# The memory's keys and values of a decoder layer: sums of squares as a row per head, roots spread by four row products, a written-out order

## The chip, the cores and the metric

The kernel runs on one core of a Trainium2 chip, in one launch. The metric is the device time of that launch in microseconds (us). A core has TensorE (PE, matrix products into PSUM banks), VectorE (DVE), ScalarE (ACT) and GpSimd (POOL) for elementwise work, and SyncE (SP), which issues most of the DMA transfers; some are issued by ACT. Each engine works through its own list of instructions in order, and semaphores tie the lists together.

## The reference, cut to what matters

One step of a decoder layer for a prompt of 1024 tokens and eight sample sequences of 4 tokens. The layer has a mixer (gated MLP beside latent attention), a cross-attention into 256 memory tokens with 4 heads of 128, and a gated convolutional FFN. The change lies where the memory's keys and values are made, between the sample's latent attention and the mixer's output projection:

```python
def mem_kv(mem, g_mem_in, w_mk, w_mv, g_mk):
    hm = rms_norm(mem, g_mem_in)                        # over 1024 features
    k = rms_norm((hm @ w_mk).reshape(n, m, 4, 128), g_mk)   # over 128, per head
    v = (hm @ w_mv).reshape(n, m, 4, 128)
# both are outputs, too; around it stand
s = masked scores of the sample's queries over 4096 cached latents, softmax, o = p @ latents
out = concat(rms_norm(a_out), rms_norm(b_out)) @ w_o
```

All is float32. A product that must keep float32's accuracy is made of three: each operand is split into a high part (a cast by ACT) and a low part (the difference, by DVE), and PE adds high*high, low*high and high*low.

## The kernel before

`phase2b` does the sample's attention over 8 batches of 16 pairs of cache pages (128 pairs, numbered by `n`). For a pair PE makes scores, ACT squares them, DVE and POOL form norms. A batch's softmax runs in 14 steps (`batch_softmax`, `r` = 0 to 13) behind its scores, then comes its product with the latents ("PV", `quad_pv`, 67 records of 257 columns) and its sums over pairs (`fold`, `oo`, `batch_out`, `batch_close`), which leave the attention's output as `olT`. `steps(n0, n1)` issues what is due in steps `n0` to `n1 - 1`, `at(n, pos, f)` adds to it; `late` holds those softmax steps of the last batch that are due behind the last score (`last` = 128).

Up to the last score the order on PE, ACT, DVE and POOL is written out by hand. Behind it only SP's is (`manual_schedule(engines={E.SP})`); a list scheduler that works with estimated costs orders the other four engines. `mem_kv` is a generator that the stage advances between pieces of the last batch's softmax. Its work, in this order:
- four heads of keys: `b` (PSUM) gets 24 records of 256 columns for a head, from 8 slices of the head's weights (`wk0`, then `stream`ed tiles `hi`, `lo`) and 8 slices of the memory tokens (`mh`, `ml`). The memory's raw tokens lie in two `ck` tiles. Head 0's loop splits them, ACT the high parts and DVE the low ones, 128x256 at a time. ACT copies each head to `kr` and its squares to `sq`;
- the memory's own sums of squares: ACT squares the raw tokens, DVE reduces 128x1024 to 128x256 twice (`acc`);
- the values `v0`, `v1` (PSUM), each 4 x 6 records of 512 columns;
- one-column products of `sq` and `acc` with a column of ones into `st`: a token is a partition there, and a head a column. DVE makes the tokens' root `rt` (128x2) and the heads' factors `r` (128x8);
- for each head two diagonal 128x128 tiles (`diag` = `ident` times a column of `r`) and their products with ones (L1658), which spread the factors along a row over all partitions; DVE multiplies `kr` with that (L1659), and ACT issues the writes of `o_mk`. ACT scales the values to `vf` by `rt` and issues `o_mv`; `vf` is one buffer.

Then `mixed` loads the rest of the mixer's output `mix` from memory and splits it into `mx1h`/`mx1l` and `mx2h`/`mx2l` (columns 384 to 767 and the rest), and `out_proj` makes the products with `w_o` in chunks `chunk(m, c)`: `m` is one of 8 slices of output features, `c` one of three ranges of tokens (384, 384, 288 columns), 24 records each. `end` makes 32 small products of `olT` with `wuv`, whose normalised result `n` is transposed by PE (`o<-ident,n`, in `mixed_sample`) and needed for `c` = 2. The ring `raw` of three 512 KB buffers takes the raw weights and the raw mixes, each one's load waiting until the splits of the one three places before are done.

Of the kernel before, what the change touches and what calls it, by code (L numbers as in the profile page):

```python
# [13 lines left out]
P = 128  # L14
# [139 lines left out]
class Net:  # L154
# [83 lines left out]
    def rsqrt_steps(self, p, out, ss, scale, e=None, eps=EPS):  # L238
# [5 lines left out]
        x, q, y, a = (self.t(p, [P, n], d, f"rq{k}{n}", 2 if n < 100 else 1)[:w] for k, d in (("x", F32), ("h", F32), ("y", I32), ("a", F32)))  # L244
# [5 lines left out]
        for k in range(2):  # L250
            yield
            o = out if k else y
            if e is nc.vector:
# [6 lines left out]
                e.scalar_tensor_tensor(o, q, 5.0, y, ALU.add, ALU.mult)  # L260
# [918 lines left out]
    def phase2b(self):  # L1179
# [50 lines left out]
        at(last - 4, 3, lambda: self.split(*wk0, raws[0].rearrange("p (k n) -> p k n", k=8)))  # L1230
        for b in range(NB):
# [3 lines left out]
            for r, (k, pos) in enumerate(((12, 0), (13, 0), (14, 0), (14, 3) if b == NB - 1 else (15, 0), (15, 0) if b == NB - 1 else (15, 3), (16, 0), (17, 0), (17, 3), (18, 2), (19, 2), (20, 0), (21, 2), (22, 3))):  # L1235
                f = lambda b=b, r=r: self.batch_softmax(p, ppt, st[b], r, b == NB - 1)
                if n + k <= last:
                    at(n + k, pos, f)
                else:
                    late.append(f)  # L1240
# [15 lines left out]
        def steps(n0, n1):  # L1256
            for n in range(n0, n1):
# [27 lines left out]
                if 0 <= n < last:  # L1285
                    rope = (Q + 1, quads[Q + 1], st[(Q + 1) // 8]) if n % 2 and Q + 1 < NB * 8 else None
                    for f in self.pair_score(p, pp, n, quads[n // 2], st[n // 16], rope):
                        at(n + 1, -1, f)
# [12 lines left out]
        with tc.manual_schedule(engines={E.SP}):  # L1301
# [5 lines left out]
            mem = self.mem_kv(raws, wk0)  # L1307
            for f in late[:3]:
                f()
            next(mem)  # L1310
            steps(last + 1, last + 4)
            for _ in range(5):
                next(mem)
            steps(last + 4, last + 7)
            for f in late[3:]:
                f()
            for _ in range(6):
                next(mem)
            steps(last + 7, last + 16 + LAG)
            for _ in mem:  # L1320
                pass
# [140 lines left out]
    def batch_softmax(self, p, pp, s, r, final):  # L1462
# [28 lines left out]
        elif r == 4:  # L1491
            s["m"] = self.t(p, [P, 2, 32], F32, "mx", 2)
            peak(0, 0, 24)
        elif r == 5:
            s["it"] = norms(24, 32, nc.gpsimd if final else nc.vector)
# [6 lines left out]
        elif r == 8:  # L1502
            scale(nc.vector, 24, 32)
# [10 lines left out]
        elif r == 11:  # L1514
# [4 lines left out]
            if final:  # L1519
                self.less(nc.vector, s)  # L1520
# [20 lines left out]
    def batch_out(self, p, s, part, pp=None, final=False):  # L1541
        nc = self.nc
        if part == 0:
            s["oo"] = self.t(p, [P, 257], F32, "oo", 2)
            nc.scalar.copy(s["oo"], s["o"])
# [33 lines left out]
    def mem_kv(self, raws, wk0):  # L1579
# [7 lines left out]
        mh, ml = (self.t(p, [P, 8, 256], FR, x) for x in ("mh", "ml"))  # L1587
        acc = [self.t(p, [P, 256], F32, f"acc{z}") for z in range(2)]
        mr = [r.rearrange("p (k n) -> p k n", k=4) for r in raws[1:3]]
        xs = [(mh[:, k], ml[:, k]) for k in range(8)]  # L1590
        kr, sq = [], []

        for h in range(4):
            w = wk0 if h == 0 else self.stream(I["w_mk"][h], 8, raw=raws[3].rearrange("p (k n) -> p k n", k=8) if h == 1 else None)
            if h == 1:
                self.behind(self.cast, cast)
            yield
            ps = self.t(pp, [P, 512], F32, "b", 2)[:, :256]
            pairs = ((0, 0), (1, 0)), ((0, 1),)
            for z in pairs if h == 0 else (((0, 0), (0, 1)), ((1, 0),)):  # L1600
                for k in range(8):
                    if h == 0 and z is pairs[0]:
                        cast = self.split(*xs[k], mr[k // 4][:, k % 4], self.col("g_mem_in", k))
                    for a, e in z:
                        nc.tensor.matmul(
                            ps, w[a][:, k], xs[k][e], start=z[0] == (0, 0) and a + e + k == 0, stop=len(z) == 1 and k == 7
                        )
                    if h == 0 and z is pairs[0] and k % 2:
                        yield
            kr.append(self.t(p, [P, 256], F32, "kr", 4))  # L1610
            nc.scalar.copy(kr[h], ps)
            sq.append(self.t(p, [P, 256], F32, "sq", 4))
            nc.scalar.activation(sq[h], ps, AF.Square)
            yield
        for x, s2 in zip(mr, acc):
            nc.scalar.activation(x, x, AF.Square)
            nc.vector.tensor_reduce(s2, x.rearrange("p k n -> p n k"), AX.X, ALU.add)
        yield
        av = [self.t(pp, [P, 512], F32, f"v{i}") for i in range(2)]

        def values(k):
            wh, wl = (x.rearrange("p k n -> p (k n)").rearrange("p (k n) -> p k n", k=2) for x in self.stream(I["w_mv"][k // 2], 8))
            for i in range(2):
                t = slice(i * P, i * P + P)
                x = self.mm3(av[i], [tuple(x[:, t] for x in xs[k + e]) for e in range(2)],
                             [(wh[:, e], wl[:, e]) for e in range(2)], first=k == 0, last=k == 6)
                if k == 4 and i == 0:
                    self.behind(x, self.spread)

        values(0)  # L1630
        yield
        values(2)
        yield
        for h in range(4):
            for i in range(2):
                nc.tensor.matmul(st[:, 2 * h + i : 2 * h + i + 1], sq[h][:, i * P : i * P + P], self.ones[:, :1], start=True, stop=True)
# [4 lines left out]
        r2 = self.t(p, [P, 2], F32, "r2")  # L1641
        r = self.t(p, [P, 4, 2], F32, "r")
        four = lambda x: x.unsqueeze(1).broadcast_to([P, 4, 2])
        self.rsqrt(p, rt, st[:, 8:10], 1.0 / 1024)
        nc.vector.tensor_tensor(r2, rt, rt, ALU.mult)
        nc.vector.tensor_tensor(r, st[:, :8].rearrange("p (h i) -> p h i", h=4), four(r2), ALU.mult)
        rf = r.rearrange("p h i -> p (h i)")
        self.rsqrt(p, rf, rf, 1.0 / 128)
        nc.vector.tensor_tensor(r, r, four(rt), ALU.mult)
        yield  # L1650
        values(4)
        yield
        for h in range(4):
            bc = self.t(pp, [P, 512], F32, "b", 2)[:, :256]
            for i in range(2):
                dg = self.t(p, [P, P], F32, "diag", 3)
                nc.vector.tensor_scalar(dg, self.ident, r[:, h, i : i + 1], None, ALU.mult)
                nc.tensor.matmul(bc[:, i * P : i * P + P], self.ones, dg, start=True, stop=True)  # L1658
            nc.vector.scalar_tensor_tensor(kr[h], kr[h], self.col("g_mk"), bc, ALU.mult, ALU.mult)  # L1659
            nc.scalar.dma_start(O["o_mk"][h], kr[h])  # L1660
            if h == 1:
                yield
        yield
        values(6)
        for i in range(2):
            vf = self.t(p, [P, 512], F32, "vf")
            x = nc.scalar.activation(vf, av[i], AF.Copy, scale=rt[:, i : i + 1])
            if i:
                self.behind(x, self.exp)
            nc.scalar.dma_start(O["o_mv"][i * P : i * P + P], vf)  # L1670
        self.close("pskv")
# [926 lines left out]
```

## Time and profile before

| what | value |
|---|---|
| median of 3 runs | 1815.08 us (1813.99 to 1815.76) |
| the profiled execution | 1815.49 us, of which the profile's span is 1813.8 us |
| PE busy | 1791.1 us, 99% of the span |
| DVE, ACT, POOL busy | 74%, 51%, 39% |
| mean granted clock of TensorE | 0.997 |

The span runs from the first to the last instruction; 1.7 us of the execution's time lie outside. Positions below are us from the span's start. The stage of the change lies between 845.9 us (the last scores) and about 907 us (the first products of the projection's third range of tokens), and PE is the busiest engine there as everywhere. A record is one matrix instruction; it is shown with its full length, though the next starts before it ends, so the cost of a record in a row of them is the distance of two starts.

### The profile page before, as it was taken

Reading aid. Unit: us, or ns where it says so; the run is one execution under the profiler, and the core shown is the slowest. Engines: PE = TensorE matmul, PEld = TensorE weight load, DVE = VectorE, ACT = ScalarE, POOL = GpSimd, SP = SyncE. Lnnn points to the kernel's source line nnn. Section 1 sums busy time; section 2 is a strip of 40 time slices with the busy share of each in tenths; the row PEclk is TensorE's granted clock in tenths of the full one; section 3 lists DMA queues with packets and bytes.
Section 4 is the critical chain, followed back from the end, with each engine's and each line's share of the span. In section 5 each row is a group of like instructions: output and inputs, shape, how many; then the busy total and the mean of one; then the engine's idle time right before and its main releaser. Section 6 shows DMA issues by size and latency. Waiting matters only on the chain.

```text
span 1813.8 us, 39386 instructions
## 1 busy us (share of the span) xinstructions
PE 1791.1 (99%) x14259; PEld 1696.6 (94%) x14259; DVE 1347.4 (74%) x2778; ACT 921.0 (51%) x1931; POOL 705.9 (39%) x858
## 2 busy tenths in 40 slices
PE   9999999999999999999999999999999999999999
PEld 8999777769999999998899989999999999999999
DVE  7864777667678777787644678988888888878664
ACT  7335676766556555565434567433333333344442
POOL 1021656534455445453033001476677767400000
PEclk9999999999999999999999999999999999999999
DMA  8101354558876666663655255122222222584242
GB/s 324 48 18 62 118 184 129 164 164 229 226 206 191 190 186 194 178 190 125 188 157 195 97 169 181 58 95 83 72 71 83 72 83 83 163 319 150 88 147 78
DMA packets 153044, 261.06 MB, mean 144 GB/s; under 512 B 20881, under 2 KB 97394, under 8 KB 152850
## 3 DMA queue, kind: packets, MB, share of 16 engines
q1 hardware_dynamic: 151986, 257.50, 45.8%
q8 instruction: 113, 1.85, 0.5%
q10 hardware_dynamic: 864, 1.05, 0.2%
q14 instruction: 81, 0.66, 0.1%
HBM read 212.66 MB, written 45.82 MB: 143 GB/s over the span
## 4 chain that ended last, share of the span: by engine, by line
PE 77%; DVE 5%; ACT 2%; DMA 1%; issue 1%; POOL 1%; SPq 1%; DVEq 0%; ACTq 0%; POOLq 0%
PE s L185 22%; PE d L185 12%; PE b L185 8%; PE E L185 7%; PE F L185 7%; PE X L185 7%; PE A L185 3%; PE o L1046 2%; PE o L1537 2%; PE tp L1031 1%; PE tp L185 1%; PE s L1422 1%; PE tp L984 1%; PE v L185 1%; PE t L185 0%
## 5 line engine op out<-in xcount | busy, mean ns | idle before, releaser
L185 PE MATMUL s<-w2h,ch 128*128 128x256 f32 x1018 | 302.1, 297 | 0.0
L185 PE MATMUL s<-w2h,cl 128*128 128x256 f32 x1018 | 293.6, 288 | 0.0
L185 PE MATMUL s<-w2l,ch 128*128 128x256 f32 x1018 | 293.1, 288 | 0.0
L185 PEld LDWEIGHTS s<-w2h,ch 128*128 128x128 f32 x1018 | 191.6, 188 | 3.3 <-issue 2.9
L185 PEld LDWEIGHTS s<-w2h,cl 128*128 128x128 f32 x1018 | 191.4, 188 | 0.4 <-DVE rqa L257 0.4
L185 PEld LDWEIGHTS s<-w2l,ch 128*128 128x128 f32 x1018 | 191.8, 188 | 0.0
L1458 DVE TENSOR_REDUCE ss<-sq 128x16 f32<-128x1024 f32 x128 | 155.2, 1213 | 29.2 <-ACT sq L1455 29.1
L1407 POOL TENSOR_TENSOR cl<-cT,ch 128x512 fp32r<-128x512 f32 x64 | 86.2, 1346 | 197.8 <-ACT ch L1403 192.0
L1455 ACT ACTIVATE sq<-s 128x512 f32<-128x512 f32 x128 | 76.4, 597 | 72.3 <-PE s L185 72.2
L200 ACT CAST a<-brb 128x528 fp32r<-128x528 f32 x77 | 48.9, 634 | 114.7 <-PE d L185 111.2
L1452 ACT ACTIVATE sq<-s 128x512 f32<-128x512 f32 x128 | 76.6, 599 | 50.4 <-PE s L185 41.2
L201 DVE TENSOR_TENSOR a<-brb,a 128x528 fp32r<-128x528 f32 x77 | 54.3, 706 | 59.1 <-ACT a L200 58.8
L185 PE MATMUL d<-a,w 128*128 128x264 f32 x768 | 95.5, 285 | 1.2 <-DVE G L2366 1.2
L185 PEld LDWEIGHTS d<-a,w 128*128 128x128 f32 x768 | 94.3, 188 | 1.4 <-issue 1.4
L2233 POOL TENSOR_TENSOR lo<-s,hi 128x1024 fp32r<-128x1024 f32 x20 | 64.2, 3208 | 45.7 <-ACT hi L2232 45.7
L2289 ACT COPY a<-A 128x264 f32<-128x264 f32 x43 | 16.1, 375 | 120.6 <-PE A L185 114.3
L185 PE MATMUL mm<-wlo,xh 128*128 128x256 f32 (+3 forms) x272 | 77.1, 286 | 0.1
L185 PE MATMUL mm<-whi,xh 128*128 128x256 f32 (+3 forms) x272 | 77.1, 285 | 0.0
L185 PE MATMUL mm<-whi,xl 128*128 128x256 f32 (+3 forms) x272 | 76.9, 287 | 0.0
L1403 ACT CAST ch<-cT 128x512 fp32r<-128x512 f32 x128 | 73.6, 628 | 0.2 <-issue 0.2
L2355 POOL TENSOR_TENSOR cv<-cv,row 128x1056 f32<-128x1056 f32 x22 | 65.1, 2958 | 21.0 <-ACT cv L2354 21.0
L185 PE MATMUL d<-a,hi 128*128 128x264 f32 x552 | 72.0, 285 | 0.0
(802 smaller groups left out, 6371.3 us busy)
## 6 DMA issues: line engine op xcount, KB each, us to landing
cT<-cT SPq DMA_DIRECT2D x256, 160.0 KB, 2.7
ck<-ck SPq DMA_DIRECT2D x256, 144.0 KB, 3.5
raw<-w_up SPq DMA_DIRECT2D x44, 512.0 KB, 3.6
wsumd<-wsum SPq DMA_DIRECT2D x26, 512.0 KB, 3.5
actd<-cv SPq DMA_DIRECT2D x44, 264.0 KB, 2.4
brb<-actd SPq DMA_DIRECT2D x44, 264.0 KB, 5.6
wsum<-w_down SPq DMA_DIRECT2D x22, 512.0 KB, 3.7
raw<-wsumd SPq DMA_DIRECT2D x20, 512.0 KB, 3.7
```

The costliest lines, as they stand in the source:

```text
L185: x = self.nc.tensor.matmul(out, l, r, start=first and i == 0, stop=last and i == len(seq) - 1)
L200: first = {"act": nc.scalar.copy, "pool": nc.gpsimd.tensor_copy, "dve": nc.vector.tensor_copy}[eng](hi, src)
L201: low = lambda: nc.vector.tensor_tensor(lo, src, hi, ALU.subtract)
L1046: nc.tensor.matmul(u["o"][g : g + 64, o : o + m * P], s["v"][:, j, h % 4], th[:, z * P : (z + m) * P], start=j == 0, stop=b == len(banks) - 1,
L1403: nc.scalar.copy(d["h"][:, k], src[k])
L1407: (nc.vector if k else nc.gpsimd).tensor_tensor(d["l"][:, k], src[k], d["h"][:, k], ALU.subtract)
L1452: nc.scalar.activation(sq[:, 0], ps[:, :, n0 : n0 + 256], AF.Square)
L1455: nc.scalar.activation(sq[:, 1], pt.rearrange("p (e d) -> p e d", e=2), AF.Square)
L1458: yield lambda: nc.vector.tensor_reduce(s["ss"][:, g0 : g0 + 2].rearrange("p e (z h) -> p z e h", z=2), sq.rearrange("p z e (h d) -> p z e ...
L1537: nc.tensor.matmul(s["o"][j * 32 : j * 32 + 32], S[:, q * 4 + j], d["ck"][:, j, :257], start=q == 0 and j > 0, stop=q == 7)
L2233: eng.tensor_tensor(lo, src, hi, ALU.subtract)
L2355: nc.gpsimd.tensor_tensor(cv, cv, row, ALU.mult)
```

## The change

- **Order.** In `mem_kv` PE, ACT and DVE follow the order in which the code is written, as SP does; in `mixed` and the first chunks of `out_proj` PE does. `mem_kv` is no longer advanced from outside but calls the softmax steps itself (`late`, and `six`, `seven` for the steps behind the last score).
- **The memory's split.** The first four of the eight slices are split between the last scores (`mem_split`, at step `last - 1`), into a tile of the softmax (`S`) and one of the ring `ck`; the other four follow the last score. The value banks are allotted ahead of `b`, so that head 0's bank is one that pair 126 had used, not the last pair.
- **Sums.** Three DVE adds (1024, 512 and 256 wide) in place of the two reduces. The squares of a head are summed by a product with 32 columns of ones, so that a head is a group of 32 partitions of `st` and a token a column (eight products, the second four adding the memory's own sums, scaled by `unit`). Four one-column records stay for `rt`.
- **Roots and their spreading.** The reciprocal root, 11 DVE operations, is taken of 128x256 (in the four `sq` tiles) instead of 128x8. The row of a head is then spread over the partitions by one product with a column of `ident` repeated 128 times: four products in place of eight diagonals and eight products.
- **Around it.** The one-column sum of batch 6's output and its four fold records come behind head 0 and head 1. The last batch's norms go from POOL to DVE. The loads of the mixes go ahead of those of `xT`. The splits of the second weights of `w_o` are tied behind the exponential (high) and the roots (low). The `wuv` products come behind the whole `chunk(0, 1)`.

```diff
-    def mem_kv(self, raws, wk0):
+    def mem_kv(self, raws, wk0, m0, late, six, seven):
...
+        av = [self.t(pp, [P, 512], F32, f"v{i}") for i in range(2)]
+        ml, mh = (self.t(p, [P, 4, 256], FR, x) for x in ("ml", "mh"))
...
+        xs = m0 + [(mh[:, k], ml[:, k]) for k in range(4)]
...
+        def add():
+            q = [x.rearrange("p k n -> p (k n)") for x in mr]
+            for n in (1024, 512, 256):
+                x, y = q if n == 1024 else (q[0][:, :n], q[0][:, n : 2 * n])
+                nc.vector.tensor_tensor(q[0][:, :n], x, y, ALU.add)
+            return q[0][:, :256]
...
+        for f in six[:3]:
+            f()
+        for k in range(4, 8):
+            self.split(*xs[k], mr[1][:, k % 4], self.col("g_mem_in", k))
+        head(0)
+        late[0]()
+        load(1)
...
+        lows[6]()
+        acc = add()
+        load(7)
+        lows[7]()
+        self.less(nc.vector, self.final)
+        values(2, 0, 1)
+        for z in range(2):
+            for h in range(4):
+                nc.tensor.matmul(
+                    st[32 * h : 32 * h + 32, :256], self.ones[:, :32], acc if z else sq[h], start=z == 0, stop=z == 1
+                )
         for i in range(2):
-            for z in range(2):
-                nc.tensor.matmul(st[:, 8 + i : 9 + i], acc[z][:, i * P : i * P + P], self.ones[:, :1], start=z == 0, stop=z == 1)
+            nc.tensor.matmul(st[:, 256 + i : 257 + i], acc[:, i * P : i * P + P], self.ones[:, :1], start=True, stop=True)
+        late[8]()
+        values(3, 0, 1)
         rt = self.t(p, [P, 2], F32, "rt")
...
+        r = sq[3]
+        for _ in self.rsqrt_steps(p, r, st[:, :256], 1.0 / 128, eps=EPS * EPS, room=sq):
+            pass
+        self.rows = self.root
+        self.rsqrt(p, rt, st[:, 256:258], 1.0 / (1024 * unit * unit))
+        seven()
         for i in range(2):
             vf = self.t(p, [P, 512], F32, "vf")
...
+            nc.scalar.activation(vf, av[i], AF.Copy, scale=rt[:, i : i + 1])
             nc.scalar.dma_start(O["o_mv"][i * P : i * P + P], vf)
+        bc = [self.t(pp, [P, 512], F32, "b", 2) for _ in range(2)]
+        bc = [x[:, e * 256 : e * 256 + 256] for x in bc for e in range(2)]
+        for h in range(4):
+            nc.tensor.matmul(bc[h], self.ident[:, 32 * h : 32 * h + 1].broadcast_to([P, P]), r, start=True, stop=True)
+        for h in range(4):
+            nc.vector.scalar_tensor_tensor(kr[h], kr[h], self.col("g_mk"), bc[h], ALU.mult, ALU.mult)
+            nc.scalar.dma_start(O["o_mk"][h], kr[h])
...
+        def rest():
+            tail[2]()
+            load((2,))
...
-        end()
-        for m in range(10):
+        E = mybir.EngineType
+        with self.tc.manual_schedule(engines={E.SP, E.PE}):
+            chunk(0, 0)
+            rest()
+            chunk(0, 1)
+            end()
+        for m in range(1, 10):
```

On PE, where the scores end: the first piece is of before, the second of after. The `s` rows are the last pair's scores, `b<-mh,wk0` (after: `b<-S,wk0`) head 0's products.

```order
5482 L185 MATMUL s_2094_14316<-w2h_1705,cl_14192 128x256
5483 L1561 MATMUL m_14456<-fold_1084_5705,oo_14408 128x32 x2
5484 L1605 MATMUL b_14410<-mh_14394,wk0h_5692 128x256
5485 L1605 MATMUL b_14410<-mh_14394,wk0l_5693 128x256
5486 L1605 MATMUL b_14410<-mh_14394,wk0h_5692 128x256
```

```order
5481 L185 MATMUL s_2096_14325<-w2h_1705,cl_14192 128x256
5482 L1619 MATMUL b_14402<-S_14309,wk0h_5692 128x256
5483 L1619 MATMUL b_14402<-S_14309,wk0l_5693 128x256
5484 L1619 MATMUL b_14402<-S_14309,wk0h_5692 128x256
...
5499 L1619 MATMUL b_14402<-ml_14380,wk0h_5692 128x256 x4
5500 L1558 MATMUL m_14438<-oo_14392,fold_1084_5705 128x1
5501 L1619 MATMUL b_14447<-S_14309,hi_14428 128x256
```

Head 0 now follows the scores directly and begins with slices that were split before; the fold records have gone behind it.

On ACT, behind the values: before, then after. `vf` are the scaled values, `mx1h` the high parts of the mix, `oo` and `olT` the copies of the last batch's output.

```order
958 L1667 ACTIVATE vf_14775<-v_2136_14617,rt_14667 128x512
959 L1670 DMA o_mv<-vf_14775 128x512
960 L1667 ACTIVATE vf_14778<-v_2137_14618,rt_14667 128x512
961 L1670 DMA o_mv<-vf_14778 128x512
962 L204 ACTIVATE mx1h_14793<-raw_14809,cols_58 128x384 x2
...
970 L1660 DMA o_mk<-kr_14575 128x256
971 L1562 COPY olT_5703<-m_14835 128x16x4
```

```order
961 L204 ACTIVATE mx1h_14756<-raw_14791,cols_58 128x384 x2
962 L204 ACTIVATE mx1h_14756<-raw_14797,cols_58 128x384 x2
963 L1707 ACTIVATE vf_14724<-v_2101_14378,rt_14663 128x512
964 L1708 DMA o_mv<-vf_14724 128x512
965 L1707 ACTIVATE vf_14727<-v_2102_14379,rt_14663 128x512
966 L1708 DMA o_mv<-vf_14727 128x512
967 L1715 DMA o_mk<-kr_14443 128x256
968 L1715 DMA o_mk<-kr_14501 128x256
969 L1715 DMA o_mk<-kr_14537 128x256
970 L1715 DMA o_mk<-kr_14571 128x256
971 L1571 COPY olT_5703<-m_14768 128x16x4
```

The scaled values stood ahead of the mix's eight high parts and stand behind them now, so that both `vf`, both `o_mv` and all four `o_mk` lie directly ahead of `olT`.

On DVE, the same place in after; the 11 operations of the roots in the `sq` tiles (L250 to L264) end right ahead of this piece, which before held the `diag` tiles, one `kr` and the mix's low halves (`mx1l`) in turn.

```order
1549 L259 SCALAR_TENSOR_TENSOR rqa_2153_14678<-rqy_2152_14677 128x2
1550 L207 SCALAR_TENSOR_TENSOR mx1l_14757<-raw_14791,cols_58,mx1h_14756 128x384
1551 L262 TENSOR_TENSOR rqa_2153_14678<-rqa_2153_14678,rqx_2150_14675 128x2
1552 L207 SCALAR_TENSOR_TENSOR mx1l_14757<-raw_14791,cols_58,mx1h_14756 128x384
1553 L263 SCALAR_TENSOR_TENSOR rqh_2151_14676<-rqa_2153_14678 128x2
1554 L264 SCALAR_TENSOR_TENSOR rt_14663<-rqh_2151_14676,rqy_2152_14677 128x2
1555 L1714 SCALAR_TENSOR_TENSOR kr_14443<-kr_14443,cols_58,b_14730 128x256
1556 L1714 SCALAR_TENSOR_TENSOR kr_14501<-kr_14501,cols_58,b_14730 128x256
1557 L1714 SCALAR_TENSOR_TENSOR kr_14537<-kr_14537,cols_58,b_14731 128x256
1558 L1714 SCALAR_TENSOR_TENSOR kr_14571<-kr_14571,cols_58,b_14731 128x256
```

The tokens' root `rt` and, behind it, the four `kr` now follow the low halves of the third load of the mix (`raw_14791`).

## Rows read from the trace of the kernel before

**Rows 1.** The page's head and its first part: busy time and share.

```profile
span 1813.8 us, 39386 instructions
...
PE 1791.1 (99%) x14259; PEld 1696.6 (94%) x14259; DVE 1347.4 (74%) x2778; ACT 921.0 (51%) x1931; POOL 705.9 (39%) x858
```

**Rows 2.** Waits of PE, 843 to 908 us: engine, line, tile, releaser, total us.

```profile
PE b L1605 <- DVE S L1454: 1.5, 1, 1.5
PE b L1658 <- DVE diag L1657: 1.0, 3, 0.6
PE m L1508 <- DVE mx L1505: 0.4, 1, 0.4
```

**Rows 3.** Stretches: length, busy PE, PEld, DVE, ACT, POOL; then TensorE's granted clock.

```profile
867.90:870.50 2.60, 2.60 (x24) 2.52 (x22) 1.30 (x2) 1.23 (x2) 0.00 (x0) 1.00 0.83 251
871.00:874.40 3.40, 3.40 (x9) 2.65 (x9) 2.44 (x13) 1.08 (x1) 0.00 (x0) 0.50 0.44 118
```

**Rows 4.** Timeline of PE: start, length, instruction, [idle before].

```profile
845.89 0.28 PE L185 MATMUL s<-w2h,cl 128*128 128x256 f32 x1
846.01 0.53 PE L1561 MATMUL m<-fold,oo 128*128 128x32 f32 x4
848.06 0.36 PE L1605 MATMUL b<-mh,wk0h 128*128 128x256 f32 x1 [1.52 <-DVE S L1454]
...
852.34 0.28 PE L1605 MATMUL b<-mh,hi 128*128 128x256 f32 x1
```

**Rows 5.** Timeline of ACT: the memory's high parts in head 0.

```profile
846.79 3.31 ACT L204 ACTIVATE mh<-ck,cols 128x256 fp32r<-128x256 f32 x8
```

**Rows 6.** Timeline of PE: the diagonal products, and `out_proj` to `wuv`.

```profile
881.84 1.36 PE L1658 MATMUL b<-diag,ones 128*128 128x128 f32 x8
...
885.83 0.42 PE L185 MATMUL b<-mx0h,hi 128*128 128x384 f32 x1
...
890.60 0.34 PE L185 MATMUL b<-mx1h,hi 128*128 128x384 f32 x1
...
893.99 1.97 PE L1328 MATMUL m<-wuv,olT 128*32 128x64 f32 x32
...
906.61 0.43 PE L1751 MATMUL o<-ident,n 32*128 32x32 f32 x4
```

**Rows 7.** Timeline of PE: 256-column float32 products elsewhere in the kernel.

```profile
208.24 0.65 PE L1046 MATMUL o<-pth,v 128*64 128x256 f32 x4
...
1035.79 0.64 PE L1861 MATMUL st<-qsq,ones 128*32 128x256 f32 x8
```

**Rows 8.** Groups of DVE operations 256 wide: count, busy us, mean ns.

```profile
L1555 DVE TENSOR_SCALAR oo<-oo,rd 128x256 f32<-128x256 f32 x7 | 2.5, 352 | 0.2
...
L1476 DVE TENSOR_TENSOR S<-S,ss 128x256 f32<-128x256 f32 x7 | 2.9, 415 | 0.0
...
L207 DVE SCALAR_TENSOR_TENSOR ml<-ck,cols,mh 128x256 fp32r<-128x256 f32 x3 | 1.3, 487 | 0.0
```

**Rows 9.** Timeline of DVE: a weight's low half, a mix's low half.

```profile
876.25 1.23 DVE L201 TENSOR_TENSOR lo<-raw,hi 128x1024 fp32r<-128x1024 f32 x1 [2.42 <-ACT hi L200]
...
885.22 0.61 DVE L207 SCALAR_TENSOR_TENSOR mx1l<-raw,cols,mx1h 128x384 fp32r<-128x384 f32 x1
```

**Rows 10.** Timeline of ACT and its DMA issues (ACTq), 876 to 905 us.

```profile
876.53 0.69 ACT L1667 ACTIVATE vf<-v,rt 128x512 f32<-128x512 f32 x1 [0.32 <-PE v L185]
...
879.63 0.69 ACT L1667 ACTIVATE vf<-v,rt 128x512 f32<-128x512 f32 x1 [2.41 <-DMA o_mv<-vf]
...
883.11 0.34 ACTq L1660 DMA_DIRECT2D o_mk<-kr  x1
...
890.79 0.19 ACT L1562 COPY olT<-m 128x64 f32<-128x64 f32 x1
...
904.74 0.71 ACT L1748 ACTIVATE n<-raw,r 32x512 f32<-32x512 f32 x1
```

**Rows 11.** DMA issues, 860 to 900 us: size, median us to landing.

```profile
raw<-mix SPq DMA_DIRECT2D x4, 384.0 KB, 3.7
```

More of the change, by code (lines that the diff above doesn't have):

```diff
@@ L1299, in phase2b @@
             steps(-10, last + 1)
-        with tc.manual_schedule(engines={E.SP}):
+        with tc.manual_schedule(engines={E.SP, E.PE, E.Activation, E.DVE}):
             self.close("ps3")
@@ L1306, in phase2b @@
             self.wp = self.open("w", bufs=3, side="right")
[L1307 to L1321, printed above, removed]
+            six = [lambda n=n: steps(last + n, last + n + 1) for n in range(1, 7)]
+            self.mem_kv(raws, wk0, m0, late, six, lambda: steps(last + 7, last + 16 + LAG))
         self.close("p3")
@@ L1502, in batch_softmax @@
         elif r == 8:
-            scale(nc.vector, 24, 32)
+            if final:
+                if "part" not in s:
+                    s["part"] = scale(nc.vector, 24, 32)
+                    self.peak = lambda: peak(0, 0, 24)
+                    return
+            else:
+                scale(nc.vector, 24, 32)
             peak(1, 24, 33)
@@ new lines, in mem_kv, with load @@
+        kr, sq, w, lows, ps = [], [], {0: wk0}, {}, {}
+        unit = float(np.float32((EPS / 8) ** 0.5))
+        pair = lambda x: x.rearrange("p k n -> p (k n)").rearrange("p (k n) -> p k n", k=2)
+        def load(j):
+            self.lows = []
+            if j == 1:
+                w[j] = self.stream(None, 8, raw=raws[3].rearrange("p (k n) -> p k n", k=8))
+            else:
+                w[j] = self.stream(I["w_mk"][j] if j < 4 else I["w_mv"][j - 4], 8)
+            lows[j] = self.lows.pop()
+            self.lows = None
@@ L1614, in mem_kv @@
[L1614 to L1623, printed above, removed]
-                t = slice(i * P, i * P + P)
[L1625 to L1636, printed above, removed]
+            nc.scalar.activation(sq[h], ps[h], AF.Square)
+        def values(j, *ii):
+            wh, wl = (pair(x) for x in w[j + 4])
+            for i in ii:
+                t = slice(i * P, i * P + P)
+                self.mm3(av[i], [tuple(x[:, t] for x in xs[2 * j + e]) for e in range(2)],
+                         [(wh[:, e], wl[:, e]) for e in range(2)], first=j == 0, last=j == 3)
@@ new lines, in mem_kv @@
+        lows[1]()
+        load(2)
+        for f in six[3:5]:
+            f()
+        keep(0)
+        head(1)
+        late[1]()
+        lows[2]()
+        load(3)
+        for x in mr:
+            nc.scalar.activation(x, x, AF.Square, scale=unit)
+        late[2]()
+        late[3]()
+        late[4]()
+        lows[3]()
+        six[5]()
+        keep(1)
+        head(2)
+        load(4)
+        lows[4]()
+        self.peak()
+        keep(2)
+        head(3)
+        load(5)
+        keep(3)
@@ new lines, in mem_kv @@
+        values(0, 0, 1)
+        lows[5]()
+        late[4]()
+        load(6)
+        values(1, 0)
+        late[5]()
+        late[6]()
+        values(1, 1)
+        late[7]()
+        lows[6]()
[9 more added lines that the diff above has]
+                )
@@ L1644, in mem_kv @@
[L1644 to L1662, printed above, removed]
@@ L1722, in mixed, with load @@
         ws = {}
-        with self.tc.manual_schedule(engines={mybir.EngineType.SP}):
-            for c, (o, n) in enumerate(CH):
-                if c == 2:
-                    for f in tail:
-                        f()
+        def load(cs):
+            for c in cs:
+                o, n = CH[c]
                 if c < 2:
                     ws[c] = self.stream(I["w_o"][c], 8)
+                    if c:
+                        self.behind(self.cast, self.exp)
+                        self.behind(self.low, self.rows)
                 for k in range(0, 8 if c else 0, 2):
@@ L2554, in build @@
     pso = N.open("pso", space=PSUM)
-    N.out_proj(pso, po, mxs, ws, xh, xl, r3, end)
+    N.out_proj(pso, po, mxs, ws, xh, xl, r3, rest, end)
     N.x = xh, xl
```

82 lines of the change are left out of this document (41 added, 41 removed).

## The prediction

> **What bounds the kernel now.** I read the page's busy shares first: PE is busy for 1791.1 of 1813.8 us [rows 1], so a gain must shorten PE's own list or fill one of its idle stretches, and work taken from another engine counts only where PE waits for it. PE's waits come next: between 843 and 908 us it waits 1.5 us for DVE before head 0, 1.0 us for the diagonals and 0.4 us for the softmax's peak [rows 2]; a wait not listed there (for `olT`, `n`, any part of the mix) is none in the kernel before. Then the clock by stretches: at 867.9 to 870.5 PE does 24 one-column records in 2.60 us at full clock, and from 871.0 to 874.4 the granted clock is 0.50, that is 1.2 instead of 2.4 GHz, while PE is busy throughout [rows 3]. So the stage loses time in four places, all of which the change touches. The order of the changed kernel then says what the other engines put in their place.
>
> **PE's own path, in the time of the trace before.**
> - *To head 2.* The last score starts at 845.89, head 0 at 848.06, head 1 at 852.34 [rows 4]; records of 256 columns start 0.12 apart. Head 0's 24 records would take 2.9 us; before they take 4.28, since ACT needs 3.31 us for eight high parts, 0.41 each [rows 5]. In the changed kernel the wait for the bank goes, and half the splits are done. ACT makes the other four behind the last pair's squares, from about 846.6 (before 846.79, since `olT`'s copy no longer stands ahead of them) to 848.2; the last low part, 0.49 [rows 8], and the four products with low parts end head 0 at about 849.5. The sum product and the four fold records, 0.75 in all, come behind heads 0 and 1. Head 2 starts at 853.1; before, 852.34 and 2.85 for head 1 and some 0.3 of short gaps give 855.5. Gain 2.4. The splits put between the last scores cost nothing as long as ACT and DVE are waiting for scores there; four of each are 1.6 and 1.95 us, so 0 to 0.5 if they come late.
> - *Peak.* The wait of 0.4 [rows 2], with its re-start 0.55, goes, since the peak now comes from DVE early.
> - *Sums.* 24 one-column records, 2.60 us [rows 3], become four, 0.45, and 16 records for 32-row groups of 256 columns. Row L1861 is that shape: eight records in 0.64 [rows 7], so 1.15 to 1.3. Gain about 1.0.
> - *Clock.* Half of 3.40 us is lost at 0.50 [rows 3], 1.7 us. What precedes the fall is the stretch of one-column records; as most of them go, I expect no fall there. Gain 1.7, or 0.
> - *Spreading.* The stretch from 881.84 to 885.83 [rows 6] becomes four float32 products of 256 columns, eight records. No row shows a weight that is one repeated column. Bounds for a record: 0.12, the distance of two 256-column records [rows 4], and 0.32, half of a 64-row pair that takes 0.65 for four [rows 7]; so 1.0 to 2.6 for eight. Twice the 0.11 of a 128-column record in the diagonals' group is nearest: 1.75. With the sum product behind it 1.9, gain 2.1. Should the repeated column cost a slower load, each record can at worst take twice that: a loss of 1.7, kept for the range.
>
> The five make 7.75. Against that I put an allowance of 0.55 for first products that meet a low half just made: heads 2 and 3 and the first and third values each start within 0.3 us of the end of their weights' low half, which takes DVE 1.23 [rows 9]. So PE comes to `out_proj` 7.2 us earlier, at 878.65 instead of 885.83.
>
> **What stands late next.** Here the order pieces decide.
> - *DVE's roots.* Sums are ready at about 869.7; one more low half ends at about 871.0. Eleven operations of 128x256: 3 of 0.352, 3 of 0.415 and 5 of 0.487 [rows 8], 4.73, and 0.03 between each two, 5.0, against 2.2 us for the same on 128x8. They end at 876.0; PE's PV ends at 876.7, so PV hides them by 0.7. Beyond that each us costs one.
> - *DVE's keys.* The next low half (`w_o`'s second) ends at 877.3 and frees its raw buffer for the mix's third load: landing 3.7 later [rows 11], 881.1. High parts, 0.6, and two low parts of 0.61 [rows 9], with the tokens' last root operations between them: `rt` at 883.4. The four `kr`, 0.44 a step, end at 885.15. They stand ahead of PE: `chunk(0, 1)`'s first product goes into the bank that the last `kr` reads. PE needs 890.60 - 885.83 = 4.77 for `chunk(0, 0)` and the fold [rows 6], is there at 883.4 and waits 1.75. Before, the last `kr` could be late, as nothing on PE waited for it.
> - *ACT's writes.* `vf` waits for `rt` and the fourth load's high parts, 883.95, takes 0.69; the second waits 2.41 for the write of the first out of the one buffer, as before [rows 10]; 0.69 again, then one `o_mv` and four `o_mk` issues of 0.34: `olT` at 889.7. Before it came at 890.79 with the values long gone [rows 10]. PE has `chunk(0, 1)` done at 885.15 + 4.25 = 889.4: a wait of 0.4 for the 32 products, which before ran at 893.99 without one [rows 6].
> - *The sample's half of the mix.* From `olT` to the end of the scaled `n` took 905.45 - 890.79 = 14.65 before [rows 10]; behind 889.7 that is 904.4 to 904.8 with the `res` and mix splits ahead of it. The transposing product stands at 906.61 [rows 6], and 1.6 us of records later in the new order. With 5.05 left of the gain and about 0.5 lost at the third weights' low half, PE gets there at 903.65 and waits 1.1.
>
> Sum: 7.2 - 1.75 - 0.4 - 0.5 - 1.1 = 3.45. The projections behind it and the FFN have the same instructions; a list scheduler shuffles some there, worth 0 to 1 either way. The profiled execution took 1815.49; less 3.45 that is 1812.0. It lies 0.4 above the median of the runs, 1815.08; from the median the same gain gives 1811.6, and I take 1811.8.
>
> **The clock, once more.** The trace shows the full clock kept over 1.52 us of idle PE before head 0 [rows 4], and lost behind a stretch of one-column records in which PE did not idle [rows 3]. The Trainium skill, "TensorE: Matmul & The Clock Gate", section "A second HAM failure mode: psum-queue depth-cycling", says that short idles between groups of matmuls, as banks are cycled, can be frequent enough to bring the half rate back. By that rule the three new waits of 1.75, 0.4 and 1.1 us, each at the start of a bank or group, could cost what this change takes away; by the trace's one idle of that length they do not.
>
> **Rivals.**
> 1. *The new waits are smaller.* If the mix's third load lands sooner or `rt` does not wait behind it, `kr` ends up to 1.75 earlier, and so does all of ACT's chain; PE keeps 5 to 7.2. For it: these four loads are all that moves then. Against it: the order ties `rt` behind that load. Time 1808.0 to 1810.3.
> 2. *The clock falls all the same,* behind PV and the spreading, or at the new waits. 1.7 comes back: 1813.5. For it: PV's 32-column products and the idles; against it: the full clock over PV before, in all stretches but one.
> 3. *The change does not do what it says at the start:* head 0 still waits, on ACT's splits or the bank, and the peak or the low halves wait in its stead. Without 2.4 and 0.55 the gain is 0.5: 1814.6.
> 4. *Slower:* ACT's list becomes the bound of the projection. `vf`, its write, the second `vf` and five issues stand ahead of `olT`, and the high parts of the last range behind it. It decides once `olT` comes more than 3.5 us after my 889.7, for then the whole net gain is gone: two landings of 3.7 instead of the 2.41 and a mix load later by 1 to 2, as with twice the traffic. With `olT` at 894 to 897, 1815.8 to 1819. For it: eight DMAs meet there; against it: before, the same ones met and `o_mv` landed fast.
>
> **How the numbers follow.** Forecast 0.46, own range 1810.3 to 1813.0; rival 1 0.24, rival 2 0.12, rival 3 0.08, rival 4 0.10. A change under 0.2%, 3.6 us, can hardly be told from none, so faster means below 1811.45: all of rival 1 and 0.19 of the forecast's 0.46, that is 0.43. Slower means above 1818.7: 0.04 of rival 4. The rest, 0.53, is the same. Rival 1 reaches down to 1808.0, and rivals 2 and 3 up to 1814.6; below and above lie some 0.06 and 0.12.
>
> **What would show it.** Right: no PE wait before head 0 and head 1 starting near 849.8; a full clock from 868 to 876; eight spreading records in 1.7 to 1.9; PE at `out_proj` near 878.7; then waits of `b` for `kr`, of `m` for `olT` and of `o` for `n`, of 3 to 4 us together. Wrong: a listed wait of the spreading products for the roots (then DVE, not PV, ends last there), records of over 0.3 in the spreading, or none of the three waits.

## The result, and the profile after

The changed kernel takes 1819.61 us (median of 12 runs, 1816.29 to 1824.13), the kernel before 1815.65 (12 runs, 1813.17 to 1819.02): ratio 1.0027, 95% interval 1.0019 to 1.0035. It is slower, by about 4 us, where 1811.8 and a range up to 1814.6 were forecast.

The page of the changed kernel; its profiled execution took 1816.69 us:

```profile
span 1815.0 us, 39350 instructions
...
PE 1787.8 (99%) x14247; PEld 1693.6 (93%) x14247; DVE 1351.3 (74%) x2777; ACT 921.3 (51%) x1931; POOL 695.8 (38%) x844
```

PE is busy 3.3 us less than before [rows 1], yet the span is longer: PE idles more. Its waits between 838 and 912 us of the changed kernel (engine, line, tile, releaser, total us):

```profile
PE m L1330 <- ACT olT L1571: 1.6, 1, 1.6
PE b L185 <- ACT hi L200: 1.2, 1, 1.2
PE b L1619 <- ACT mh L204: 1.2, 1, 1.2
PE b L185 <- DVE kr L1714: 0.7, 1, 0.7
PE b L185 <- DVE lo L201: 0.6, 1, 0.6
PE o L1811 <- ACT n L1808: 0.6, 1, 0.6
```

They are 5.9 us together, against 2.9 before [rows 2]. All three old ones are gone, and the new ones lie later. Stretches of the changed kernel, columns as in [rows 3]:

```profile
866.00:870.50 4.50, 4.50 (x33) 3.03 (x32) 4.36 (x8) 2.03 (x2) 0.00 (x0) 1.00 0.45 112
870.50:876.50 6.00, 6.00 (x77) 3.94 (x77) 5.17 (x14) 1.84 (x5) 0.00 (x0) 1.00 0.36 102
876.50:902.40 25.90, 21.92 (x149) 20.88 (x147) 14.19 (x40) 12.54 (x27) 1.30 (x3) 1.00 0.62 196
902.50:909.30 6.80, 6.14 (x20) 5.58 (x21) 3.73 (x11) 2.59 (x7) 1.84 (x2) 0.50 0.71 195
```

The sums, the values, PV and the spreading (866 to 876.5) now run at full clock without a gap, where before had 0.50 for 3.4 us [rows 3]. In 876.5 to 902.4 PE idles 4.0 of 25.9 us, and right behind it the granted clock is 0.50 (1.2 GHz) for 6.8 us.

PE's timeline at the points that the prediction named (start, length, instruction, [idle before]). At the last score this execution was 2.9 us ahead of the one before, 2.7 of it from unchanged code, most of that because its clock did not fall near 216 us as there; so 2.9 is to be added where times are compared with [rows 4, 6].

```profile
842.96 0.28 PE L185 MATMUL s<-w2h,cl 128*128 128x256 f32 x1
...
845.34 0.39 PE L1619 MATMUL b<-mh,wk0h 128*128 128x256 f32 x1 [1.15 <-ACT mh L204]
...
847.97 0.36 PE L1619 MATMUL b<-S,hi 128*128 128x256 f32 x1
...
866.09 0.64 PE L1691 MATMUL st<-sq,ones 128*32 128x256 f32 x8
866.54 0.61 PE L1691 MATMUL st<-ck,ones 128*32 128x256 f32 x8
867.09 0.61 PE L1695 MATMUL st<-ones,ck 128*128 128x1 f32 x4
...
874.55 1.99 PE L1712 MATMUL b<-sq,ident 128*128 128x256 f32 x8
876.38 0.28 PE L1558 MATMUL m<-oo,fold 128*128 128x1 f32 x2
876.52 0.42 PE L185 MATMUL b<-mx0h,hi 128*128 128x384 f32 x1
...
882.02 0.42 PE L185 MATMUL b<-mx1h,hi 128*128 128x384 f32 x1 [0.73 <-DVE kr L1714]
...
888.03 1.97 PE L1330 MATMUL m<-wuv,olT 128*32 128x64 f32 x32 [1.58 <-ACT olT L1571]
...
901.28 0.44 PE L185 MATMUL b<-mx0h,hi 128*128 128x384 f32 x1 [1.17 <-ACT hi L200]
...
902.54 0.69 PE L185 MATMUL b<-mx0h,lo 128*128 128x384 f32 x1 [0.64 <-DVE lo L201]
...
905.12 0.63 PE L1811 MATMUL o<-ident,n 32*128 32x32 f32 x4 [0.62 <-ACT n L1808]
```

Head 0 follows the last score directly, the eight spreading records take 1.83 from start to start, and `out_proj` begins at 876.52, 879.4 on the axis of before: 6.4 us earlier than 885.83 [rows 6]. From there to 925 us 8.2 us are given back: the five waits from `kr` to `n`, 4.74, and half of 6.8 at the half clock, 3.4.

The three lists on which those waits hang, all of the changed kernel. ACT first:

```profile
844.78 1.71 ACT L204 ACTIVATE mh<-ck,cols 128x256 fp32r<-128x256 f32 x4 [0.90 <-DVE kss L1418]
...
881.43 0.67 ACT L1707 ACTIVATE vf<-v,rt 128x512 f32<-128x512 f32 x1
...
884.20 0.69 ACT L1707 ACTIVATE vf<-v,rt 128x512 f32<-128x512 f32 x1 [2.10 <-DMA o_mv<-vf]
...
885.30 2.42 ACTq L1715 DMA_DIRECT2D o_mk<-kr  x4
887.77 0.21 ACT L1571 COPY olT<-m 128x64 f32<-128x64 f32 x1 [2.88 <-issue]
...
900.18 1.04 ACT L200 CAST hi<-raw 128x1024 fp32r<-128x1024 f32 x1 [3.23 <-DMA raw<-w_o]
```

Then DVE:

```profile
880.22 1.65 DVE L1714 SCALAR_TENSOR_TENSOR kr<-kr,cols,b 128x256 f32<-128x256 f32 x4
...
882.85 0.55 DVE L1827 TENSOR_TENSOR res<-b,res 128x384 f32<-128x384 f32 x1
890.32 0.56 DVE L201 TENSOR_TENSOR xl<-res,xh 128x384 fp32r<-128x384 f32 x1 [6.92 <-DMA o_mk<-kr]
890.79 2.60 DVE L207 SCALAR_TENSOR_TENSOR mx2l<-raw,cols,mx2h 128x288 fp32r<-128x288 f32 x6
...
901.26 1.23 DVE L201 TENSOR_TENSOR lo<-raw,hi 128x1024 fp32r<-128x1024 f32 x1 [2.82 <-ACT hi L200]
```

And SP's DMA queue, the four loads of the mix's last range and the third weights:

```profile
883.43 0.33 SPq L1828 DMA_DIRECT2D res<-res  x1
883.86 8.26 SPq L1781 DMA_DIRECT2D raw<-mix  x4
892.18 1.41 SPq L1824 DMA_DIRECT2D res<-xT  x3
893.70 0.36 SPq L1580 DMA_DIRECT2D raw<-w_o  x1
```

`xl`, the low part of the residual, lies in memory that `vf` and `kr` had, so DVE stands still for 6.92 us, by the trace until the last `o_mk` is written. Behind it stand the low parts `mx2l` that free the raw ring, so the third weights of `w_o` are asked for at 893.70 only, 896.6 on the axis of before. The same queue of the kernel before:

```profile
885.14 6.81 SPq L1734 DMA_DIRECT2D raw<-mix  x4
892.06 0.40 SPq L1768 DMA_DIRECT2D res<-res  x1
...
897.14 1.18 SPq L1571 DMA_DIRECT2D raw<-w_o  x2
```

PE is some 4 us earlier than there behind the `wuv` products, the weights' load 0.5. And the first `res` write, which waits for `chunk(0, 0)`, stands ahead of the mix loads now and stood behind them before.

### The profile page after: what moved, and what is told of

Its sections match the earlier page's. It is cut to its first block, busy times and chain, and to the rows that moved or that the text cites. A ratio compares the mean times of both kernels' runs of the same rounds, so it can differ in the third digit from the quotient of the medians.

```text
span 1815.0 us, 39350 instructions
## 1 busy us (share of the span) xinstructions
PE 1787.8 (99%) x14247; PEld 1693.6 (93%) x14247; DVE 1351.3 (74%) x2777; ACT 921.3 (51%) x1931; POOL 695.8 (38%) x844
## 4 chain that ended last, share of the span: by engine, by line
PE 74%; DVE 7%; ACT 3%; DMA 2%; issue 2%; SPq 1%; ACTq 0%; DVEq 0%; POOL 0%
PE s L185 22%; PE d L185 12%; PE b L185 7%; PE E L185 6%; PE F L185 6%; PE X L185 6%; PE A L185 3%; PE o L1546 2%; PE o L1050 1%; PE tp L1035 1%; PE tp L185 1%; PE s L1424 1%; PE v L185 1%; PE b L1619 1%; PE tp L988 1%
```

## The experiments

Theory A: PE's own path shrank as forecast, and the waits on ACT's, DVE's and SP's lists behind 880 us gave it back, partly by bringing the clock down. Theory B: the gain itself is missing or lost elsewhere. A ratio is against the kernel before on the same chip; its medians there were 1814.27 (the first four kernels below), 1815.50 (the next four) and 1815.52 (the last two).

**The changed kernel again** (`e0_again`), without an edit.

> The changed kernel as it is, once more, to tell what of its profile repeats. Theory A (the loss is made by waits between 880 and 905 us, on ACT's and DVE's lists, which also bring TensorE's clock down right behind them): the waits for olT (1.6), for the third weights of w_o (1.2 + 0.6) and for n (0.6) return within 0.5 each, and a half-rate stretch begins within 5 us of the last of them; about 1819.5. Theory B (the stage itself gains; the loss is a half-rate stretch at about 1585 us and a longer wait for G there, brought by the list scheduler's other order in the FFN): the waits are small or vary, and the FFN's stretch returns with 1.9 us; also about 1819.5. What returns in both profiles is the kernel's; what does not is chance.

1817.74, ratio 1.0019 [1.0007, 1.0030]. Its waits in the stage are 6.5 us together (`hi` 1.8, `olT` 1.2, `mh` 1.2, `n` 1.0, `vf` 0.7, `lo` 0.6), and the clock is 0.50 from 905.5 for 6.8 us. So both repeat; the stretch at the half clock near 1585 us did not return.

**Two `vf` buffers** (`e1_vf2`), so that the second value needn't wait for the first one's write.

```diff
-            vf = self.t(p, [P, 512], F32, "vf")
+            vf = self.t(p, [P, 512], F32, "vf", 2)
```

> The changed kernel with two buffers for vf instead of one, so that the second scaled value does not wait for the first one's write (2.1 us on ACT). Theory A: olT's copy comes 2.1 earlier, the wait of 1.6 for it goes, the four writes of o_mk leave 2.1 earlier, DVE's stall behind them ends 2.1 earlier and the third weights come earlier by as much; the waits between 880 and 905 shrink from 4.0 to about 1 and the half-rate stretch there goes: 3 to 6 us less than the changed kernel, 1814 to 1816. Theory B: within 1 us of the changed kernel, unless the FFN's order differs.

1815.61, 1.0004 [0.9992, 1.0015]: 2.1 less than the changed kernel beside it, not the 3 to 6 expected. The waits for `olT` and for `mh` are gone, `hi` 1.8, `kr` 0.8, `lo` 0.6 and `n` 0.6 stay, and so does the half clock (6.8 us from 904). The second buffer also moves what is allotted behind it. In the changed kernel ACT's `mh` waits for DVE's `kss`, which it does not read; `kss` reads `ksq`, the last pair's squares, so the likely reason is that `mh` lay in the memory of `ksq`. No run shows the addresses, but that wait, the 1.15 us in head 0, is there in every kernel with one `vf` buffer and in none with two. The edit is therefore two in one.

**`xl` in eight tiles** (`e2_xl`) instead of one, so that it no longer waits for all writes of `kr` and `vf`.

```diff
-    xh, xl = (N.t(xp, [P, 8, NT], FR, n) for n in ("xh", "xl"))
+    xh = N.t(xp, [P, 8, NT], FR, "xh")
+    xl = Slices(N.t(xp, [P, NT], FR, f"xl{k}") for k in range(8))
```

> The changed kernel with the low half of the projected tokens (xl) in eight tiles of one slice each instead of one tile. The first slice then shares no memory with kr or vf and need not wait for their writes to land (DVE stood idle for 6.9 us there). Theory A: the low halves of the mix's last range come 4 to 6 us earlier, so the raw buffers are free earlier and the third weights of w_o land before PE wants them; the waits of 1.2, 0.6 and 0.6 go, the one for olT (1.6) stays, and the half-rate stretch near 902 goes: 4 to 6 us less than the changed kernel, 1813.5 to 1815.5. Theory B: within 1 us of it, unless the FFN's order differs.

1814.19, 0.9998 [0.9989, 1.0008], 3.5 less than the changed kernel beside it. `hi` falls to 0.6 and `olT` to 0.4, `kr` (2.0) and `n` (1.5) grow; no half clock in the stage. DVE's wait before `xl` is down to 3.85 us and is now one for ACT's cast of `xh`. The waits of the stage add up to 6.3 us, no less than before the edit, so in this profile the gain lies in the clock and not in shorter waits.

**Both edits together** (`e3_vf2_xl`).

> Both: two buffers for vf and xl in eight tiles. Theory A: none of the waits for olT, w_o's third weights and n; only the wait for kr (0.7) and the first one for the memory's high parts (1.2) are left, so the stage keeps about 5.5 us of its gain: 1810 to 1812. Theory B: 1817 to 1819.5, as the loss lies elsewhere.

1813.50, 0.9993 [0.9982, 1.0004]. Waits: `n` 1.5, `kr` 0.8, `lo` 0.6, `hi` 0.6; half clock for 3.4 us from 903.1. The edits don't add up to their single effects.

**Both, and the last range's mix loads ahead of the first `res` write** (`e4_vf2_xl_rest`) on SP.

```diff
+            if (m, c) == (0, 0):
+                rest()
             nc.sync.dma_start(self.res_dram[:, m, o : o + n], res)
...
             chunk(0, 0)
-            rest()
             chunk(0, 1)
```

> Two buffers for vf, xl in eight tiles, and on SP's queue the four loads of the mix's last range ahead of the first write of res instead of behind it. Theory A (waits between 880 and 910 us decide): that write stood until DVE had added the first chunk (882.4 to 886 in the runs so far), and the loads behind it began only then, though two of their buffers had long been free; now the first two leave some 3 us earlier, the third weights of w_o come about 3 us earlier, and the waits for them (0.6 + 0.6) and for n (1.5) go: 2 to 3 us less than with vf and xl alone, about 1811, and no half-rate stretch near 903. Theory B (the load was not bound by that queue, but by the landing of what is split before): unchanged, about 1813.5.

1814.24, 0.9988 [0.9979, 0.9997]. That fell short: `hi` 1.2, `n` 1.8, `kr` 0.8 and `lo` 0.6 remain, since now the second `res` write (894.05) stands ahead of the weights' load (894.42). The half clock, expected to go, is there for 3.4 us from 905.0.

**That order of SP alone** (`e6_rest`) in the changed kernel.

> The changed kernel with SP's order alone mended (the last range's mix loads ahead of the first write of res); vf has one buffer and xl is one tile, as in the changed kernel. Theory A: the loads leave 3 us earlier, and by the list order the low halves of the mix now stand ahead of xl on DVE, so that its wait of 6.9 us for o_mk's writes no longer holds them; the waits for w_o's third weights and for n (2.4 to 3.4 together) go, the one for olT stays, the half-rate stretch near 903 goes or is halved: 4 to 6 us less than the changed kernel, 1812.5 to 1815. Theory B: at most 1 us less, as DVE still waits for the writes.

1816.71, 1.0012 [1.0003, 1.0021]; less than expected. `hi` falls from 1.2 to 0.7, `n` grows to 1.8, the half clock is halved (3.4 us from 906.6). On DVE the low halves do stand ahead of `xl` now, as theory A said:

```profile
889.44 2.60 DVE L207 SCALAR_TENSOR_TENSOR mx2l<-raw,cols,mx2h 128x288 fp32r<-128x288 f32 x6 [4.81 <-ACT mx2h L204]
891.96 0.55 DVE L201 TENSOR_TENSOR xl<-res,xh 128x384 fp32r<-128x384 f32 x1
```

But they wait 4.81 us for ACT's high parts, which stand behind the writes and `olT`'s copy (888.76) on ACT, and the weights' load follows the second `res` write on SP again (895.84 behind 895.47).

**A pad tile ahead of `mh`** (`e7_pad`), meant to move it off `ksq`.

```diff
+        self.t(p, [P, 512], F32, "pad")
         ml, mh = (self.t(p, [P, 4, 256], FR, x) for x in ("ml", "mh"))
```

> The changed kernel with 2 KB left free in front of ml and mh. With two buffers for vf the first wait of the stage (1.2 us for the memory's high parts, which stood behind a reduce on DVE) was gone too, since mh had moved to other addresses. If the wait was one for memory that an earlier tile's reader still held, it goes here as well: 1.2 us less than the changed kernel, or 0.5 to 2 with what the clock makes of it. If it was ACT's or DVE's order, it stays, and so does the time.

1819.34, 1.0023 [1.0013, 1.0033]. `mh` kept its wait of 1.2, so the pad did not do what it was meant to, and nothing was tested; with the same instructions in the same order, it is a third measurement of the changed kernel. Its profiled execution, 1812.49, is the fastest of its 11 runs. It had waits at the same six places, 6.1 us together (`olT` 1.6, `n` 1.4, `mh` 1.2, `kr` 0.7, `lo` 0.6, `hi` 0.6), and no stretch at the half clock at all. So the same program has the fall in one run and not in another.

**Useless products in the idle places** (`e5_fill`): 16 records of 384 columns on PE, 8 ahead of the `wuv` products, 8 ahead of `chunk(2, 0)`. The products that follow start their banks afresh; some ties that keep the order there are left out of the diff.

```diff
+            if (m, c) == (2, 0):
+                filler(ps, 1, 8)
...
             chunk(0, 1)
+            filler(self.t(self.ppt, [P, 512], F32, "o", 1)[:, :384], 0, 8)
             end()
```

> The changed kernel with 16 records of 384 columns added on PE whose results are thrown away: eight ahead of the wuv products, where PE waits 1.2 to 1.6 us for olT, and eight ahead of the first product with w_o's third weights, where it waits 1.2 to 1.8. They take 1.4 us each, so they lie in waits that are there anyway. Theory A1 (idle PE at these places brings TensorE's clock down there): the half-rate stretch of 6.8 us at 902 to 906 goes or is halved; 1.5 to 3.4 us less than the changed kernel, in spite of 3 us more work. Theory A2 (the waits alone cost the time, the half rate is set off by something else, such as the small products): the stretch stays and the time is the same to 1 us longer.

1815.35, 0.9999 [0.9987, 1.0011]: some 4 us less than the changed kernel against the same before (1819.34 and 1.0023 for `e7_pad`, on the same chip), though PE has 16 records more to do. The waits for `olT`, `hi`, `lo` and `n` have gone, and the stretch that was at the half clock is now (columns as above):

```profile
902.50:909.30 6.80, 6.80 (x44) 6.51 (x43) 4.45 (x12) 3.79 (x10) 2.02 (x2) 1.00 0.67 206
```

The filled idles cost nothing, as PE would have waited there, and the clock does not fall behind them. The one wait of this kernel left in the projection, 2.0 us for `kr`, has a half-rate stretch of 3.4 us right behind it (885.3). Over all runs the mean granted clock is 0.9982, against 0.9958 to 0.9965 of the changed kernel's three series. That is 1.7 to 2.4 thousandths of 1813 us, or 3.1 to 4.3 us, uncertain by about 1 from the scatter of the runs: the clock accounts for the difference.

**Both edits, and the first two `res` writes issued by ACT** (`e8_queue`) behind its cast of `xh`; SP loads `xT` first, then all mixes.

```diff
-            nc.sync.dma_start(self.res_dram[:, m, o : o + n], res)
+            if m or c == 2:
+                nc.sync.dma_start(self.res_dram[:, m, o : o + n], res)
...
+            if m == 0 and c < 2:
+                nc.scalar.dma_start(self.res_dram[:, m, o : o + n], res)
...
             chunk(0, 0)
-            rest()
+            rest[0]()
             chunk(0, 1)
+            rest[1]()
```

> Two buffers for vf, xl in eight tiles, and the writes of res of the first two chunks issued by ACT behind its own cast of the same res, so that on SP no write stands ahead of the mix's loads of the last range or of w_o's third weights; xT's loads for both chunks go first. With the mix loads ahead of the writes the third weights still waited, since the second write stood ahead of them on SP until DVE had added the second chunk. Theory A (the queue's order decides when the third weights land): they leave at about 888 to 890 instead of 894.4, land before PE wants them, and the root of the sample's output no longer stands behind their low half on DVE; the waits for hi (1.2), lo (0.6) and n (1.8) go, only that for kr (0.8) stays; no half rate between 880 and 910. Stage about 3 us shorter than with the earlier edits: 1810.5 to 1812.5. Theory B (the landings of the mixes and the ring of three raw buffers decide): at most 1 us shorter, and the waits stay.

1812.01, 0.9981 [0.9971, 0.9991]. One wait is left in the stage, since the third mix load now comes later:

```profile
PE b L185 <- DVE kr L1714: 2.9, 1, 2.9
```

and right behind it, at 885.7, the clock falls (two neighbouring stretches):

```profile
883.00:885.70 2.70, 0.22 (x1) 0.25 (x2) 2.70 (x9) 1.90 (x4) 0.00 (x0) 1.00 0.37 95
885.70:889.10 3.40, 3.40 (x12) 3.40 (x12) 1.17 (x3) 0.93 (x4) 0.18 (x1) 0.50 0.88 270
```

**The same, with the four `kr` ahead of the third mix load's low halves** (`e9_krs`) on DVE.

```diff
-            nc.vector.scalar_tensor_tensor(kr[h], kr[h], self.col("g_mk"), bc[h], ALU.mult, ALU.mult)
+            self.krs = nc.vector.scalar_tensor_tensor(kr[h], kr[h], self.col("g_mk"), bc[h], ALU.mult, ALU.mult)
...
+                        elif k + e == 4:
+                            self.behind(self.low, self.krs)
```

> The same, and on DVE the four kr ahead of the low halves of the mix's third load, which they had to wait for. The wait of PE for kr (0.8) goes, and nothing that PE needs comes later, since the third load's low halves are used 2 us later: 0.5 to 1 us less than the kernel with the queue's order alone, 1809.5 to 1812. If that wait comes back elsewhere (for mx1l), no difference.

**1809.33** (6 runs, 1807.97 to 1810.06), 0.9967 [0.9954, 0.9979]: 6.2 us faster than before, so it beats both kernels. No wait of PE is listed between 838 and 912 us. Its stretches, for those of the changed kernel above:

```profile
876.50:902.40 25.90, 25.90 (x173) 24.99 (x173) 18.93 (x55) 16.62 (x37) 3.06 (x4) 1.00 0.81 253
902.50:909.30 6.80, 6.80 (x44) 6.80 (x43) 3.88 (x7) 2.79 (x7) 1.05 (x1) 1.00 0.57 175
```

PE is busy throughout, with 173 records where the changed kernel had 149, at full clock. Against before, its unchanged code runs 0.3 us late at 800 us and 7.1 early from 900 on: the stage gains 7.4, nearly the 7.2 that the prediction had for PE's own path. So the gain itself is there once the waits are gone, and theory B is out for the stage.

By the mean clocks idle PE makes the fall likelier, but it does not make it certain. Of the ten profiles of kernels with waits in this stage, eight have a stretch at the half clock there, 6.8 us in three (the changed kernel, `e0_again`, `e1_vf2`) and 3.4 in five; `e2_xl` and `e7_pad`, with 6.3 and 6.1 us of waits, have none, nor has `e9_krs` without waits. And the kernel before had one in which PE did not idle [rows 3].

## Why the prediction was wrong

The mechanism on PE's path was right; what it set free was mispriced, in three terms of "What stands late next" and in the clock. The step that failed most is the clock's: the sum has nothing for a fall at the new waits, since one idle of that length had kept the full clock, and in two of three profiles of this program it cost 3.4 us. Next are the third weights' 0.5, which measured 1.81, and the wait of 0.4 for `olT`, which measured 1.58.

- *To head 2, peak, sums, clock at 871, spreading.* Forecast 7.2 with the allowance, measured 6.4 in the changed kernel and 7.4 without waits (`e9_krs`). The 16 sum records took 1.00 where 1.15 to 1.3 was taken, the four one-column records 0.47 (forecast 0.45), spreading 1.83 where 1.75 was taken; the clock did not fall from 866 to 876. DVE's eleven root operations took 4.7 us (forecast 5.0), and PV hid them. What was short is head 0: "ACT makes the other four from about 846.6" came out at 847.7 on that axis, behind `kss` (0.90 us of waiting on ACT). Rival 3 had named "waits on ACT's splits", but it came for 1.15 of its 2.95.
- *DVE's keys.* Forecast a wait of 1.75, measured 0.73. The four `kr` ended at 884.8 on the axis of before (forecast 885.15); PE came later than forecast.
- *ACT's writes.* `olT` at 890.7 instead of 889.7, a wait of 1.58 instead of 0.4. The short term is "four `o_mk` issues of 0.34": the four, back to back, took 2.42, some 0.60 each, and 1.91 to 2.45 in the other runs. The one of 0.34 in [rows 10] stood alone. Why a row of them costs more isn't shown.
- *The sample's half of the mix.* "About 0.5 lost at the third weights' low half" measured 1.17 + 0.64. This is the term that was not worked out: nothing in it looked at what SP has to pass (the first `res` write ahead of four mix loads) or at what `xl`'s memory held. `n` was done at 908.0 on that axis, some 3.2 us later than forecast, since its root stands behind that low half on DVE; PE was late too, so its wait was 0.62 instead of 1.1.
- *The clock.* Rival 2 had it at 1.7 us and a chance of 0.12, "at the new waits". It took 3.4 in each of two profiles, and in the third nothing. The prediction had one idle of 1.52 us that kept the full clock [rows 4], and let that one row decide. Against it stood the Trainium skill, "TensorE: Matmul & The Clock Gate", section "A second HAM failure mode: psum-queue depth-cycling", by which short idles between groups of matmuls can be frequent enough to bring the half rate back. The runs agree with that rule on the average and not run by run: with the idles filled (`e5_fill`) or gone (`e9_krs`) the mean clock is 0.9982 and 0.9980, against 0.9958 to 0.9965, but two profiles (`e2_xl`, `e7_pad`), each with some 6 us of waits, kept the full clock in the stage.

By terms, in the changed kernel's profile: given back 8.14 instead of 3.75, of which `kr` -1.02, `olT` +1.18, third weights +1.31, `n` -0.48 and the clock +3.40. Rival 4 forecast nearly this time, 1815.8 to 1819, but by `olT` more than 3.5 us late, and it was 1.0; it isn't what happened.

The median moved by 4.0. Against the one profile of before, which itself lost 1.7 to the clock in this stage, the stage is 1.6 longer in this profile, 2.1 longer in the second, and 0.8 shorter in the third, without the fall. In the two series that list the clock of both kernels over all runs, it is 0.9965 against 0.9972 (`e0_again`) and 0.9960 against 0.9973 (`e7_pad`), which stands for 1.2 of 3.5 us and 2.4 of 3.8, each uncertain by about 1. The rest, 1.4 to 2.3, is lost at full clock: the waits of the stage, 5.9 to 6.5 in three profiles, against the saved work. Part of it may lie in the FFN, where this profile has a wait for `G` of 2.0 against 1.2 before, but the other two profiles of the same program have 1.3 and 1.5. How it divides isn't settled. Nor is what made the clock fall at 1585 us in this profile, far behind the change.

## What to carry to other kernels

When PE's path gets shorter, walk every in-order list that feeds the next stage at the new time: each DMA issue in front of the copy that matters, each write that stands ahead of a load on the same queue, and each tile that reuses the memory of one still being written out. Waits of PE of a microsecond or two, close together, are to be priced at their length and with a chance of a half-rate stretch behind them. A version that only gets rid of the waits is worth trying before the change is dropped: here four small edits to lists and buffers turned 4 us lost into 6 us gained.

## What the runs showed of the hardware that was not expected

- A product whose weights are one column repeated 128 times (L1712) shows no slower load: eight records of 256 columns took 1.83 us, 0.23 each, about twice the 0.11 that the prediction read for 128 columns of the diagonals.
- The 16 sum records into four groups of 32 rows (L1691) took 1.00 us, 0.06 each, where a record of L1712, also of 256 float32 columns, took 0.23: four of them, one into each group, cost about as much as one of those.
- The same program, in three profiled executions (the changed kernel, `e0_again`, `e7_pad`), had 6.8 us at half clock at 902.5, 6.8 us at 905.5, and none. A fall like this one has a price only as an average over runs.
